# A new DRAM layout for the dense gates and for three weight matrices of an encoder block

## The chip, the core and the metric

One core of a Trainium2 chip runs the whole kernel in one launch. The metric is the device time of one execution in microseconds. TensorE (PE) multiplies, VectorE (DVE) and ScalarE (ACT) do the elementwise work, GpSimd (POOL) issues the gathers, SyncE (SP) issues the plain DMAs, and 16 DMA engines move the bytes of both queues: q0 holds what POOL issues, q1 what SP issues.

## The reference

The block takes 1024 tokens of width 1024 in float32:

```
h = rmsnorm(x, g_mix);  q, k, v, u, gv = split(h @ w_in)          # w_in 1024 x 2560
o = diff_attention(q, k, v)           # 4 heads, block-causal, softmax(1) - lam * softmax(2)
y = spatial_gating(gelu(u), gelu(gv)) # 128-position blocks, lower-triangular w_s
x = x + concat(o, y) @ w_out          # w_out 1024 x 1024
xn = rmsnorm(x, g_ffn)
s = (xn @ w_q) . sub_keys             # w_q 1024 x 2048; 8 heads x 2 halves x 128 keys
top 16 of each half -> top 16 pairs per head -> 128 (expert, gate) pairs per token of 16384 experts
x = x + sum_e gate_e * gelu(w_u[e] . xn) * w_v[e]
return rmsnorm(x, g_final)
```

## The kernel before

Tokens are eight blocks of 128, taken in four passes of two blocks. A front part (`front`) does everything up to the selection of experts. For each pass, stage A is the combined projection with `w_in`, B attention, M/Y the spatial gating, D the projection with `w_out` (line 509), S the queries with `w_q` (line 544) and the top 16 of each half, and t the selection of the pairs. Weights come in pieces of 128 partitions by 2 by 512 floats, 512 KB each, through a ring of three tiles (`pieces`, line 300): 80 loads of `w_in`, 32 of `w_out`, 64 of `w_q`.

The expert layer is done in two ways. Blocks 0, 1, 6 and 7 gather: 128 rows of `w_u` and then 128 rows of `w_v` for each token, one indirect DMA of 128 rows of 4 KB per pair index (line 664), and one DVE instruction of 1024 columns behind each (lines 685 and 699). Blocks 2 to 5 (512 tokens) are dense: all 16384 experts are multiplied, in 128 steps of 128 experts (`dense`), and a dense gate matrix picks those that were chosen.

The dense gates are built by `gates`, called G1 for blocks 2 and 3 and G2 for blocks 4 and 5. For each token two one-hot matrices (DVE lines 626 and 641, ACT lines 645 and 646) are multiplied on PE (line 650); ACT copies four tokens at a time into a tile `st` of 128 partitions by 128 expert columns by 16 tokens (line 651), and after four such copies SP stores `st` to the DRAM tensor `gd` (line 652). There are 32 stores of 1 MB, 16 in G1 and 16 in G2. G1 has one `st` tile and two `oh1` tiles, G2 has three `st` tiles (dictionaries G1 and G2, lines 46 and 47).

In `dense`, `gd` comes back in 16 loads of 2 MB into `gg` (line 750), one for each eight steps, double buffered. Each step loads 512 KB of `w_uT` (`ur`, line 757) and 512 KB of `w_v` (`vr`, line 777), splits both into a high and a low float32r part on ACT and DVE, makes `hp` on PE (lines 765 to 767), applies gelu and the gate (line 771) and accumulates the outputs (lines 743 to 745). Before it, four loads bring the transposed tokens into `xl` (line 724), and ACT and DVE split them (lines 726 and 727).

The order on each engine is fixed when the program is built: a scheduler interleaves the gathers with the front and with the dense steps, and every engine then runs its list in order and waits where it must. The `w_u` rows of blocks 0 and 1 and the `w_v` rows of block 0 are gathered in the front, the other gathers run beside the dense steps, and what is left of them after the last dense step is a tail.

Of the kernel before, what the change touches and what calls it, by code (L numbers as in the profile page):

```python
# [7 lines left out]
F32 = mybir.dt.float32  # L8
# [10 lines left out]
P = 128  # L19
# [19 lines left out]
TB = 16  # L39
NTB = TD // TB  # L40
GRP = 4
# [20 lines left out]
def peer_block(tc, d):  # L62
    nc = tc.nc
    dve, act, pe, pool, sp = nc.vector, nc.scalar, nc.tensor, nc.gpsimd, nc.sync

    with ExitStack() as ctx:
        E = ctx.enter_context
        cp = E(tc.tile_pool(name="consts", bufs=1))
        dram = E(tc.tile_pool(name="scratch", bufs=1, space=DRAM))
# [25 lines left out]
        S = {}  # L95
# [35 lines left out]
                                             op0=ALU.mult, op1=ALU.subtract)  # L131

        x1_d = [dram.tile([P, D], F32, name=f"x1_{b}") for b in range(NB)]
        gd = dram.tile([P, NTB, P, TB], F32, name="gd")
        xT_d = dram.tile([P, DC, TD], F32, name="xT_d")
        sel_t = {}
        rs2_t = {}
# [91 lines left out]
        def front():  # L229
# [151 lines left out]
            def stage_a(p, order):  # L381

                blocks = PASSES[p]
                nt = len(blocks) * P
                t0 = blocks[0] * P
                if ("xT", p) not in S:
                    S["xT", p] = norm_x(p)
                xT = S["xT", p]

                def natural(c):  # L390
                    ps = project(xT, lambda q: d["w_in"][:, q * 2:q * 2 + 2, c * 512:(c + 1) * 512], f"wi{p}_{c}", blocks)
                    for i, b in enumerate(blocks):
                        if c == 2:
                            act.activation(vv[b], ps[i], AF.Copy)
                        else:
                            t = a2.tile([P, 512], F32, name=f"ug{c}_{b}", tag=f"ug{c}", bufs=UG[c])
                            act.activation(t, ps[i], AF.Gelu_apprx_tanh)
                            S[c, b] = t
                def transposed(c):
                    ps = [accp.tile([P, 512], F32, name=f"qk{p}_{c}_{i}", tag="acc") for i in range(2)]  # L400
                    src = lambda q: d["w_in"][:, q * 2:q * 2 + 2, c * 512:(c + 1) * 512]
                    for dc, w in pieces(src, f"wi{p}_{c}", xT[1] is None):
                        for h in range(NH):
                            o_ = ps[h // 2][:, (h % 2) * nt:(h % 2) * nt + nt]
                            mm(o_, cut(w, slice(None), slice(h * P, (h + 1) * P)), cut(xT, slice(None), dc, slice(0, nt)),
                               dc == 0 and h % 2 == 0, dc == DC - 1, skip_group_check=True)
                    if c == 0:
                        S["q", p] = a2.tile([P, NH, PW * P], F32, name=f"qT{p}", tag="qT")
                        for h in range(NH):
                            act.activation(S["q", p][:, h, :nt], ps[h // 2][:, (h % 2) * nt:(h % 2) * nt + nt], AF.Copy,  # L410
                                           scale=HD ** -0.5 / SLOPES[h])
                    else:
                        for h in range(0, NH, 2):
                            act.activation(kT[:, h:h + 2, t0:t0 + nt],
                                           ps[h // 2][:, :2 * nt].rearrange("p (a b) -> p a b", a=2), AF.Copy)
                for c in order:
                    if c == "g":
                        gmlp(p, accp, "acc")
                    elif c in "01":
                        transposed(int(c))  # L420
                    else:
                        natural(int(c))
# [78 lines left out]
            def stage_d(p):  # L501

                blocks = PASSES[p]
                x1 = {b: f4.tile([P, D], F32, name=f"x1_{b}", tag="x4k") for b in blocks}
                for b in blocks:
                    sp.dma_start(x1[b], d["x"][b * P:(b + 1) * P, :])
                for hf in range(2):
                    hs = slice(hf * 512, (hf + 1) * 512)
                    ps = project(S["mT", p], lambda q: d["w_out"][:, q * 2:q * 2 + 2, hs], f"wo{p}_{hf}", blocks)
                    for i, b in enumerate(blocks):  # L510
                        dve.tensor_tensor(x1[b][:, hs], x1[b][:, hs], ps[i], ALU.add)
                sT = pair(f"sT{p}", f"S{p}")
                ms = sm.tile([P, PW], F32, name=f"ms2_{p}", tag="ms")
                for i, b in enumerate(blocks):
                    sp.dma_start(x1_d[b], x1[b])
                    jk = f2.tile([P, D], BF16, name=f"jk2_{b}", tag="jk", bufs=1)
                    act.activation(jk, x1[b], AF.Square, accum_out=ms[:, i:i + 1])
                rs2 = sel.tile([P, PW], F32, name=f"rs2_{p}", tag="rs2")
                dve.tensor_copy(rs2, rsqrt(ms, PW, 1.0 / D, f"rf{p}", sm))
                for i, b in enumerate(blocks):  # L520
                    rs2_t[b] = rs2[:, i:i + 1]
                    act.activation(x1[b], x1[b], AF.Copy, scale=rs2_t[b])
                    pp, tag = (accp, "acc") if p == len(PASSES) - 1 else (smp, "smp")
                    transpose_split(x1[b], gffn, sT[0], sT[1], i, pp, tag, f"sT{b}")
                S["sT", p] = sT
                if blocks[0] in DENSE:
                    c0 = DENSE.index(blocks[0]) * P
                    sp.dma_start(xT_d[:, :, c0:c0 + PW * P], sT[0])

            def stage_s(p):  # L530
# [8 lines left out]
                def query(c):  # L539

                    kt = f2.tile([P, 4, P], F32, name=f"kt{p}_{c}", tag="kt")
                    sp.dma_start(kt, d["keys"][:, c * 4:(c + 1) * 4, :])
                    ps = [accp.tile([P, 512], F32, name=f"pq{p}_{c}_{i}", tag="acc") for i in range(2)]
                    src = lambda q: d["w_q"][:, q * 2:q * 2 + 2, c * 512:(c + 1) * 512]
                    for dc, w in pieces(src, f"sc{p}_{c}", T[1] is None):
                        for q in range(4):
                            mm(ps[q // 2][:, (q % 2) * nt:(q % 2) * nt + nt], cut(w, slice(None), slice(q * P, (q + 1) * P)),
                               cut(T, slice(None), dc, slice(0, nt)), dc == 0 and q % 2 == 0, dc == DC - 1, skip_group_check=True)
                    qT = f2.tile([P, 4, PW * P], F32, name=f"sq{p}_{c}", tag="sq")
                    for q in range(0, 4, 2):  # L550
                        act.activation(qT[:, q:q + 2, :nt], ps[q // 2][:, :2 * nt].rearrange("p (a b) -> p a b", a=2), AF.Copy)
                    return kt, qT
# [45 lines left out]
        def gates(blocks, pp, tag, bufs):  # L598
# [7 lines left out]
            for b in blocks:  # L606
# [7 lines left out]
                for c in range(P // TB):  # L614
                    ci = bi * (P // TB) + c
                    st = g1.tile([P, P, TB], F32, name=f"st{ci}", tag="st", bufs=bufs["st"])
                    for t0 in range(0, TB, 4):
# [31 lines left out]
                        for j in range(4):  # L649
                            pe.matmul(pg[:, j * P:(j + 1) * P], oh2[:, j, :], oh1[:, j, :], start=True, stop=True)  # L650
                        act.activation(st[:, :, t0:t0 + 4], pg.rearrange("p (t i) -> p i t", t=4), AF.Copy)  # L651
                    sp.dma_start(gd[:, ci], st)
            gs.close()

        ring = [0]
# [53 lines left out]
        def dense():  # L709
# [37 lines left out]
            for gi in range(NG):  # L747
                if gi % 2 == 0:
                    gg = d2.tile([P, NTB, 2 * GRP, TB], F32, name=f"gg{gi}", tag="gg")
                    sp.dma_start(gg, gd[:, :, gi * GRP:(gi + 2) * GRP, :])  # L750
                vh = d1.tile([P, GRP, D], F32R, name=f"vh{gi}", tag="vh")
                vl = d1.tile([P, GRP, D], F32R, name=f"vl{gi}", tag="vl")
                av = []
# [67 lines left out]
def _layouts(inputs):  # L821

    import numpy as np
    c = np.ascontiguousarray

    def chunked(a):

        return c(a.reshape(-1, P, a.shape[-1]).transpose(1, 0, 2))
    i = {k: np.asarray(v) for k, v in inputs.items()}
    r = {}  # L830
    r["x"] = c(i["x"].reshape(NT, D))
    r["w_in"] = chunked(i["w_in"][0])
    r["w_out"] = chunked(i["w_out"][0])
    r["g_mix"] = c(i["g_mix"][0].reshape(DC, P).T)
    r["g_ffn"] = c(i["g_ffn"][0].reshape(DC, P).T)
    r["g_ffn_row"] = c(i["g_ffn"][0])
    r["g_final"] = c(i["g_final"])
    r["g_gv"] = c(i["g_gv"][0])
    r["g_subln"] = c(i["g_subln"][0].reshape(P, 1))
    r["g_gout"] = c(i["g_gout"][0].reshape(4, P).T)  # L840
    r["b_s"] = c(i["b_s"][0].T)
    r["lam"] = np.concatenate([i["lam_q1"][0], i["lam_k1"][0], i["lam_q2"][0], i["lam_k2"][0]])
    r["w_s"] = c(i["w_s"][0].transpose(2, 0, 1))
    r["w_q"] = chunked(i["peer_wq"][0])
    r["keys"] = c(i["peer_keys"][0].reshape(16, P, P).transpose(2, 0, 1))
    r["w_u"] = c(i["peer_wu"][0])
    r["w_v"] = c(i["peer_wv"][0])

    r["w_uT"] = c(i["peer_wu"][0].reshape(P, P, DC, P).transpose(0, 3, 2, 1).reshape(P, P, D))
    return r  # L850
# [19 lines left out]
```

## Time and profile before

| | us |
|---|---|
| median of 3 runs | 2809.84 |
| lowest, highest | 2806.77, 2818.14 |
| profiled execution | 2825.71 |
| its span, first to last instruction | 2823.9 |
| PE busy | 2423.6 (86%) |
| DVE busy | 2404.8 (85%) |
| ACT busy | 1000.3 (35%) |
| POOL busy | 1488.8 (53%) |
| DMA q0 (gathers), share of 16 engines | 53.0% |
| DMA q1 (SP's loads and stores), share of 16 engines | 33.2% |

A share over the whole span mixes stages with different limits, so the profile is to be read by stage. The front lasts to about 1300 us, the dense steps from there to about 2707 us, the tail to the end.

### The profile page before, as it was taken

How to read it: one execution, taken by the hardware profiler on the slowest of the kernel's cores; microseconds unless marked ns; L12 is line 12 of the kernel's file. 1: busy time of each engine (PE TensorE's matmuls, PEld its weight loads, DVE VectorE, ACT ScalarE, POOL GpSimd, SP SyncE). 2: the span in 40 equal slices, each digit the busy share in tenths (PEclk: the TensorE clock that was granted, in tenths of full speed). 3: DMA queues.
4: the chain of work that ended last, by engine and by line, in shares of the span. 5: the costliest groups of instructions: out<-in, count | busy, mean ns of one | idle time of the engine just before them, and what ended most of it. 6: DMA issues, size and time to landing. Idle time of an engine off the chain costs nothing.

```text
span 2823.9 us, 33571 instructions
## 1 busy us (share of the span) xinstructions
PE 2423.6 (86%) x10764; PEld 1909.5 (68%) x10764; DVE 2404.8 (85%) x5223; ACT 1000.3 (35%) x2063; POOL 1488.8 (53%) x1139
## 2 busy tenths in 40 slices
PE   6789997995569774797999999999999999999930
PEld 5575655753447542695887887888888888888820
DVE  4448867999988999999898887987888978888998
ACT  5553322224553542983323232232232322323300
POOL 5362564356655325321265646655566657655665
PEclk9799998996569777898999999999999999999965
DMA  5266999998899858797699999999999989998998
GB/s 174 59 181 184 343 365 359 337 339 297 299 348 331 295 182 290 264 366 247 214 346 350 352 322 366 354 333 342 328 356 343 342 306 384 349 359 303 331 333 343
DMA packets 316514, 869.56 MB, mean 308 GB/s; under 512 B 26033, under 2 KB 93745, under 8 KB 312241
## 3 DMA queue, kind: packets, MB, share of 16 engines
q0 software_dynamic: 149760, 545.33, 53.0%
q1 hardware_dynamic: 166576, 322.09, 33.2%
q8 instruction: 85, 1.39, 0.2%
q14 instruction: 93, 0.75, 0.1%
HBM read 823.28 MB, written 44.04 MB: 307 GB/s over the span
## 4 chain that ended last, share of the span: by engine, by line
PE 61%; DVE 19%; DMA 10%; issue 5%; ACT 4%; POOL 1%; SPq 0%; DVEq 0%; ACTq 0%; POOLq 0%
PE hp L765 7%; PE hp L767 7%; PE hp L766 7%; PE y L745 6%; PE y L743 6%; PE y L744 6%; PE pq L309 5%; DVE y L699 4%; DVE u L685 4%; DMA u<-in_w_u_dram,idx 3%; PE pgg L650 2%; PE wi L309 2%; PE op L743 2%; PE op L745 2%; PE op L744 2%
## 5 line engine op out<-in xcount | busy, mean ns | idle before, releaser
L664 POOL DMA_INDIRECT v<-in_w_v_dram,idx x512 | 664.9, 1299 | 656.5 <-DVE y L699 321.2
L664 POOL DMA_INDIRECT u<-in_w_u_dram,idx x512 | 700.1, 1367 | 530.7 <-DVE h L685 226.7
L699 DVE SCALAR_TENSOR_TENSOR y<-v,a,y 128x1024 f32<-128x1024 f32 x512 | 656.3, 1282 | 15.8 <-DMA v<-in_w_v_dram,idx 9.0
L685 DVE CUSTOM_DVE_ANT_0 u<-u,xn 128x1024 f32<-128x1024 f32 x512 | 614.2, 1220 | 50.6 <-DMA u<-in_w_u_dram,idx 50.2
L765 PE MATMUL hp<-xh,uh 128*128 128x512 f32 x1024 | 400.0, 391 | 22.0 <-ACT xh L726 15.6
L766 PE MATMUL hp<-xl,uh 128*128 128x512 f32 x1024 | 399.3, 390 | 2.4 <-DVE xl L727 2.4
L767 PE MATMUL hp<-xh,ul 128*128 128x512 f32 x1024 | 399.3, 390 | 0.6 <-DVE ul L761 0.6
L778 ACT ACTIVATE vh<-vr 128x1024 fp32r<-128x1024 f32 x128 | 130.7, 1052 | 510.8 <-PE op L745 481.1
L744 PE MATMUL y<-vl,ah 128*128 128x512 f32 x768 | 298.8, 389 | 0.0
L743 PE MATMUL y<-vh,ah 128*128 128x512 f32 x768 | 298.8, 389 | 0.0
L745 PE MATMUL y<-vh,al 128*128 128x512 f32 x768 | 287.6, 389 | 2.2 <-DVE al L775 2.2
L650 PE MATMUL pgg<-oh,oh 128*128 128x128 f32 x1024 | 190.3, 344 | 102.7 <-ACT st L651 63.9
L650 PEld LDWEIGHTS pgg<-oh,oh 128*128 128x128 f32 x1024 | 170.3, 247 | 132.6 <-ACT st L651 84.0
L765 PEld LDWEIGHTS hp<-xh,uh 128*128 128x128 f32 x1024 | 192.7, 188 | 64.4 <-ACT xh L726 15.8
L766 PEld LDWEIGHTS hp<-xl,uh 128*128 128x128 f32 x1024 | 192.7, 188 | 43.0 <-DVE xl L727 3.1
L767 PEld LDWEIGHTS hp<-xh,ul 128*128 128x128 f32 x1024 | 192.6, 188 | 41.4 <-DVE ul L761 1.4
L760 ACT ACTIVATE uh<-ur 128x1024 fp32r<-128x1024 f32 x128 | 135.1, 1056 | 168.7 <-PE hp L766 149.7
L761 DVE TENSOR_TENSOR ul<-ur,uh 128x1024 fp32r<-128x1024 f32 x128 | 156.3, 1221 | 36.6 <-ACT uh L760 36.5
L309 PE MATMUL pq<-sT,sc 128*128 128x256 f32 x768 | 184.0, 389 | 0.7 <-ACT sT L127 0.7
L779 DVE TENSOR_TENSOR vl<-vr,vh 128x1024 fp32r<-128x1024 f32 x128 | 153.5, 1220 | 16.3 <-ACT vh L778 16.3
L745 PEld LDWEIGHTS y<-vh,al 128*128 128x128 f32 x768 | 144.2, 188 | 33.3 <-DVE al L775 3.5
L309 PEld LDWEIGHTS pq<-sT,sc 128*128 128x128 f32 x768 | 143.8, 195 | 32.8 <-issue 10.7
(440 smaller groups left out, 4117.2 us busy)
## 6 DMA issues: line engine op xcount, KB each, us to landing
ur<-in_w_uT_dram SPq DMA_DIRECT2D x128, 512.0 KB, 6.5
vr<-in_w_v_dram SPq DMA_DIRECT2D x128, 512.0 KB, 6.5
wi<-in_w_in_dram SPq DMA_DIRECT2D x80, 512.0 KB, 5.0
sc<-in_w_q_dram SPq DMA_DIRECT2D x64, 512.0 KB, 6.4
gd<-st SPq DMA_DIRECT2D x32, 1024.0 KB, 7.2
gg<-gd SPq DMA_DIRECT2D x16, 2048.0 KB, 21.8
wo<-in_w_out_dram SPq DMA_DIRECT2D x32, 512.0 KB, 7.0
x<-in_x_dram SPq DMA_DIRECT2D x16, 512.0 KB, 6.5
```

Source lines behind the costliest of these rows:

```text
L309: pe.matmul(ps, s_[i], m_[j], start=first and n == 0, stop=last and n == len(ops) - 1, **kw)
L650: pe.matmul(pg[:, j * P:(j + 1) * P], oh2[:, j, :], oh1[:, j, :], start=True, stop=True)
L664: pool.indirect_dma_start(out=t, out_offset=None, in_=d[src], in_offset=bass.IndirectOffsetOnAxis(ap=ix, axis=0))
L685: dve.tensor_tensor_reduce(t, t, xn, 1.0, 0.0, ALU.mult, ALU.add, h[:, j:j + 1])
L699: dve.scalar_tensor_tensor(y, t, a[:, j:j + 1], y, op0=ALU.mult, op1=ALU.add)
L743: pe.matmul(ps, ah[:, bs], vh[:, hs], start=first, stop=False, skip_group_check=True)
L744: pe.matmul(ps, ah[:, bs], vl[:, hs], start=False, stop=False, skip_group_check=True)
L745: pe.matmul(ps, al[:, bs], vh[:, hs], start=False, stop=last, skip_group_check=True)
L761: dve.tensor_tensor(ul, ur, uh, ALU.subtract)
L765: pe.matmul(hp[:, :TD], uh[:, ds_], xh[:, dc, :], start=(dc == 0), stop=False)
L766: pe.matmul(hp[:, :TD], uh[:, ds_], xl[:, dc, :], start=False, stop=False)
L767: pe.matmul(hp[:, :TD], ul[:, ds_], xh[:, dc, :], start=False, stop=(dc == DC - 1))
```

## The change

Only the order of bytes in DRAM changes. In `gd` the expert columns are grouped by eight: one partition's data for one load of `gg` lies in one run of 16 KB, where it was 32 runs of 512 B. The store of `st` writes 16 runs of 512 B for each partition, 16 KB apart, where it wrote one run of 8 KB. `w_in`, `w_out` and `w_q` are laid out on the host so that one load reads 4 KB per partition in one run, where it read two runs of 2 KB. The number of DMAs and the bytes of each stay as they were.

```
-        gd = dram.tile([P, NTB, P, TB], F32, name="gd")
+        gd = dram.tile([P, P // (2 * GRP), NTB, 2 * GRP, TB], F32, name="gd")
...
-                    ps = project(xT, lambda q: d["w_in"][:, q * 2:q * 2 + 2, c * 512:(c + 1) * 512], f"wi{p}_{c}", blocks)
+                    ps = project(xT, lambda q: d["w_in"][:, c, q * 2:q * 2 + 2, :], f"wi{p}_{c}", blocks)
...
-                    ps = project(S["mT", p], lambda q: d["w_out"][:, q * 2:q * 2 + 2, hs], f"wo{p}_{hf}", blocks)
+                    ps = project(S["mT", p], lambda q: d["w_out"][:, hf, q * 2:q * 2 + 2, :], f"wo{p}_{hf}", blocks)
...
-                    src = lambda q: d["w_q"][:, q * 2:q * 2 + 2, c * 512:(c + 1) * 512]
+                    src = lambda q: d["w_q"][:, c, q * 2:q * 2 + 2, :]
...
-                    sp.dma_start(gd[:, ci], st)
+                    sp.dma_start(gd[:, :, ci], st.rearrange("p (a b) t -> p a b t", b=2 * GRP))
...
-                    sp.dma_start(gg, gd[:, :, gi * GRP:(gi + 2) * GRP, :])
+                    sp.dma_start(gg, gd[:, gi // 2])
...
-    def chunked(a):
-
-        return c(a.reshape(-1, P, a.shape[-1]).transpose(1, 0, 2))
+
+    def tiled(a):
+
+        return c(a.reshape(-1, P, a.shape[-1] // 512, 512).transpose(1, 2, 0, 3))
...
-    r["w_in"] = chunked(i["w_in"][0])
-    r["w_out"] = chunked(i["w_out"][0])
+    r["w_in"] = tiled(i["w_in"][0])
+    r["w_out"] = tiled(i["w_out"][0])
...
-    r["w_q"] = chunked(i["peer_wq"][0])
+    r["w_q"] = tiled(i["peer_wq"][0])
```

No instruction moves on any engine. SP's list at the end of G2 and the entry of the dense part, in the changed kernel (a row is a line of the kernel, the tile written, the tile read, and the shape of the transfer):

```order
L652 DMA gd<-st_8550 2048x1x128
L300 DMA sc_3_2_9019<-in_w_q_dram 128x1024
L707 DMA out_dram<-y_18507 128x1024
L542 DMA kt_3_8995<-in_keys_dram 128x512
L300 DMA sc_3_3_9029<-in_w_q_dram 128x1024
L750 DMA gg_9219<-gd 128x4096
L757 DMA ur_9223<-in_w_uT_dram 128x1024
L777 DMA vr_9261<-in_w_v_dram 128x1024
L757 DMA ur_9265<-in_w_uT_dram 128x1024
L777 DMA vr_9303<-in_w_v_dram 128x1024
L750 DMA gg_9761<-gd 128x4096
L724 DMA xl<-xT_d 128x1024 x4
```

The kernel before has the same rows in the same places; the shapes there are 128x2048 for `gd<-st`, 128x2x512 for the `sc` loads and 128x32x128 for `gg<-gd`. Two loads of `gg` stand ahead of the loads of `xl`, in both.

## Rows read from the trace of the kernel before

**Rows 1.** Windows by stage: length, engines' busy us (instructions), clock, DMA share, GB/s.

```profile
0.00:240.00 240.00, 188.70 (x1048) 157.19 (x1049) 115.44 (x509) 124.82 (x303) 115.67 (x100) 0.88 0.47 139
240.00:500.00 260.00, 234.95 (x840) 146.87 (x839) 203.31 (x616) 79.51 (x211) 130.20 (x104) 0.95 0.92 332
680.00:1040.00 360.00, 268.58 (x1150) 199.13 (x1151) 325.72 (x888) 178.22 (x477) 174.01 (x139) 0.74 0.84 298
1130.00:1270.00 140.00, 122.91 (x766) 111.40 (x765) 138.41 (x362) 123.50 (x330) 45.03 (x38) 0.94 0.88 314
1270.00:1300.00 30.00, 12.18 (x68) 10.23 (x66) 29.79 (x156) 8.87 (x12) 1.81 (x1) 0.72 0.99 328
1300.00:2707.00 1407.00, 1397.51 (x6142) 1153.14 (x6142) 1221.06 (x1637) 407.54 (x522) 811.41 (x577) 1.00 0.92 331
2707.00:2824.00 117.00, 0.00 (x0) 0.00 (x0) 106.24 (x109) 5.64 (x10) 69.86 (x67) 0.51 0.89 349
```

**Rows 2.** DVE's waits for gathers, 1300 to 2710: total us, times, longest.

```profile
DVE u L685 <- DMA u<-in_w_u_dram,idx: 10.6, 14, 1.5
DVE y L699 <- DMA v<-in_w_v_dram,idx: 6.8, 3, 5.5
```

**Rows 3.** Two links of the chain, dense part: start, us, what.

```profile
1483.46 20.03 DMA vr<-in_w_v_dram
...
1739.56 23.75 DMA ur<-in_w_uT_dram
```

**Rows 4.** PE's wait at the dense entry (us, times, longest); DVE there, by time.

```profile
PE hp L765 <- ACT xh L726: 15.6, 1, 15.6
...
1299.49 1.28 DVE L727 TENSOR_TENSOR xl<-xl,xh 128x512 fp32r<-128x512 f32 x2
```

**Rows 5.** The page's DMA issues: count, size, median us from issue to landing.

```profile
ur<-in_w_uT_dram SPq DMA_DIRECT2D x128, 512.0 KB, 6.5
...
wi<-in_w_in_dram SPq DMA_DIRECT2D x80, 512.0 KB, 5.0
sc<-in_w_q_dram SPq DMA_DIRECT2D x64, 512.0 KB, 6.4
gd<-st SPq DMA_DIRECT2D x32, 1024.0 KB, 7.2
gg<-gd SPq DMA_DIRECT2D x16, 2048.0 KB, 21.8
wo<-in_w_out_dram SPq DMA_DIRECT2D x32, 512.0 KB, 7.0
```

**Rows 6.** Windows: 1 KB stores, 8 KB stores, 512 B loads, 4 KB gathers.

```profile
465.00:472.00 7.00, 7.00 (x34) 6.17 (x33) 3.11 (x16) 3.52 (x5) 3.45 (x3) 1.00 0.94 291
1002.00:1004.00 2.00, 2.00 (x11) 1.15 (x10) 2.00 (x5) 1.25 (x5) 0.46 (x1) 1.00 1.02 426
1290.00:1295.00 5.00, 0.00 (x0) 0.00 (x0) 5.00 (x25) 0.00 (x0) 0.00 (x0) 0.50 0.93 273
...
2720.00:2800.00 80.00, 0.00 (x0) 0.00 (x0) 78.42 (x74) 1.82 (x4) 58.32 (x56) 0.50 0.97 378
```

**Rows 7.** The chain from 230 to 500 us, shares by line.

```profile
by line: PE wi L309 13.7%; DMA u<-in_w_u_dram,idx 9.6%; PE qk L309 8.0%; DMA wi<-in_w_in_dram 6.5%; DVE u L685 6.0%; DMA wo<-in_w_out_dram 5.9%; PE s L444 5.6%; PE wo L309 5.0%; DMA x<-x 4.5%; PE pq L309 4.5%; issue 2.7%; PE ops L477 2.2%; 
```

**Rows 8.** G1's stores, 680 to 1040: issues, who waited, landing; DVE's wait for PE.

```profile
L652 SPq DMA_DIRECT2D gd<-st x16: 319/326/418, 682.5 to 1034.4; - x16
...
  ACT st L651: 26.9, 9
...
DMA to landing us min/median/max: 3.8/7.4/9.1
...
DVE oh L641 <- PE pgg L650: 4.7, 5, 1.4
```

**Rows 9.** G2's stores, 1130 to 1270: issues and landing.

```profile
L652 SPq DMA_DIRECT2D gd<-st x16: 319/324/460, 1133.4 to 1260.2; - x16
...
DMA to landing us min/median/max: 3.8/7.0/14.1
```

More of the change, by code (lines that the diff above doesn't have):

```diff
@@ L400, in transposed @@
                     ps = [accp.tile([P, 512], F32, name=f"qk{p}_{c}_{i}", tag="acc") for i in range(2)]
-                    src = lambda q: d["w_in"][:, q * 2:q * 2 + 2, c * 512:(c + 1) * 512]
+                    src = lambda q: d["w_in"][:, c, q * 2:q * 2 + 2, :]
                     for dc, w in pieces(src, f"wi{p}_{c}", xT[1] is None):
```

## The prediction

> **What bounds the kernel now.** I read the windows by stage first, since the shares of the whole span hide the stages. From 1300 to 2707 us PE is busy 1397.5 of 1407 us at the full clock [rows 1]: the dense steps are bound by PE, and 9.5 us of idle PE is all that any other engine or transfer takes there. From 2707 on PE has nothing and DVE is busy 106 of 117 us [rows 1]: the tail is the gathers left over, at DVE's pace. Before 1300 the picture changes. From 680 to 1300 DVE leads, with 325.7 of 360, 138.4 of 140 and 29.8 of 30 us [rows 1]. From 240 to 500 no engine is full, PE 235 and DVE 203 of 260 us, while the DMA engines are at 0.92. From 0 to 240 the DMA engines are at 0.47 and nothing is full [rows 1].
>
> The DMA share invites a wrong reading: 0.92 over the whole dense part looks like a bound. Whether it is one is seen in DVE's waits for gathers. They come to 10.6 and 6.8 us in 1410 us [rows 2], and the number of gathers left for the tail is fixed by DVE's list, not by how early they land. So spare bandwidth beside the dense steps buys at most those 17.4 us, and only where the wait holds up PE or the tail.
>
> **The change, part by part.** All 224 transfers (176 weight loads, 32 stores and 16 loads of `gd`) stay in their places on SP; only the sizes of their pieces change. So each part is a price per transfer, then what of it reaches the path.
>
> Prices. The share and the rate of a short stretch give what the 16 engines would move if full. In the tail 4 KB pieces move at 378 GB/s with a share of 0.97, so 390; 512 B loads at 273 with 0.93, so 294; 1 KB stores (`xT_d`) at 291 with 0.94, so 310; 8 KB stores of `gd` (the one issued at about 1001 us) at 426 with 1.02, so 418 [rows 6]. The first 240 us, where most loads have 2 KB pieces, give 139 / 0.47 = 296 [rows 1].
>
> (a) Weights, 176 loads of 0.524 MB. 1.77 us of the DMA engines each at 296 GB/s, 1.34 at 390: 0.43 us less. In the first 240 us the engines stand idle half the time; I take 1 us there, for the loads that begin the chain. From 230 to 500 the chain holds 6.5% + 5.9% of waiting for `wi` and `wo`, 33 us of 270 [rows 7]. If these landed faster in the ratio of the two rates, 24%, that would be 8 us; but a load of the same size that comes in 4 KB pieces already, `ur`, takes 6.5 us to land, against 5.0, 6.4 and 7.0 for `wi`, `sc` and `wo` [rows 5], so most of a landing is not piece size. I take 2 us. Against a gain stands that larger pieces give q1 a larger part of the busy engines, and the gathers beside it a smaller one. Sum -3 us; bounds -10 and +3.
>
> (b) Stores of G1. The store in 512 B pieces is not in the trace. Nearest rows: 1 KB stores at 310 and 512 B loads at 294 GB/s, so 1.05 MB takes 3.4 to 3.6 us of full engines, against 2.5 at 418: +1.0 us. Beside gathers it is worse: a `gg` load in 512 B pieces lands in 21.8 us for twice the bytes, 10.9 per MB, against 7.2 for a `gd` store [rows 5], +3.7. G1 has one `st` tile, so ACT's first copy of the next 16 tokens waits for the store. Queued behind that copy are ACT's next one-hots, PE's next gate product and what stands behind it on PE. Now 9 of 16 stores hold ACT up, 26.9 us in all, while DVE waits only 4.7 us for gate products [rows 8], about 17%. The cushion: the stores come every (1034.4 - 682.5) / 15 = 23.5 us, 5.9 for a group of four tokens, and two `oh1` tiles let DVE be up to two groups ahead, 11.7 us. With +1.0 to +3.7 us on 16 stores ACT waits 16 to 59 us more; 17% of it is 3 to 10. I take +5 us; bounds 0 (all in the cushion) and +20 (a third comes through).
>
> The Trainium skill has a rule for this price (DMA: Bandwidth & Descriptors, section Why small descriptors are slow): each packet costs a fixed three cycles or so beside its 32-byte beats. An estimate from that page: 19 cycles for 512 B, so 152 for 4 KB in eight pieces, against 131 in one, 16% more. The trace does not agree in size: 390 against 294 GB/s is 33% [rows 6]. By the page's figure the store would cost 0.4 us more instead of 1.0, and this term +2.
>
> (c) Stores of G2. 16 stores in 126.8 us, one every 8.5 us, and three tiles, so a tile is wanted again after about 25 us while a store lands in 7.0, at most 14.1 [rows 9]: no wait. The engines are what is short: they are busy 0.88 x 140 = 123 us [rows 1], and the stores add 16 x 1.0 = 16, about all that is free. The `sc` loads in the same queue feed PE and, through the top 16, DVE, which has 1.6 us of idle time in 140. I take +2 us; bounds -2 (the `sc` loads gain more than the stores cost) and +11.
>
> (d) Entry of the dense part. PE stands still for 15.6 us until ACT has `xh` [rows 4], and two `gg` loads are queued ahead of `xl`. Each needs 2.1 MB / 294 = 7.1 us of full engines, and 5.4 at 390: `xl` could land 3.5 us earlier. It helps little, since the second product needs the low part from DVE, and DVE is busy 29.8 of the 30 us before it takes it up at 1299.5 in its own order [rows 1, 4]. The last store lands later by 1 to 4 us, ahead of all this. I take 0; bounds -3.5 and +3.
>
> (e) Dense steps. The 14 other `gg` loads keep q1 for about 20 us each; a `ur` or `vr` behind one lands after 20.0 or 23.8 us instead of 6.5, and the chain runs through it [rows 3, 5]. With 16 KB pieces `gg` has the larger part of the engines and should be through in half the time. Of the 9.5 us of idle PE I take back 4; bounds 0 and -9.5. What hides the rest of the saved DMA time is PE's own work, at 99%.
>
> (f) Tail: no `gg`, no weights, DVE's pace. 0.
>
> Sum: -3 + 5 + 2 + 0 - 4 = 0, against the profiled execution's 2825.7 us (span 2823.9). The runs shown have a median of 2809.84, 15.9 us lower; the sum carries over as a difference: 2810 us. The ends add to -25 and +37.
>
> **The rivals.**
>
> Faster: the dense part is bound by DMA after all. For it: a share of 0.92 with gathers in flight all the time. 16 loads give back 16 x (7.1 - 5.4) = 27 us of DMA time, and DVE's 17.4 us of waiting for gathers [rows 2] would go and come off the tail, as its list runs ahead. Against it: PE at 99%. Time: 2810 - 17 = 2793 us.
>
> Slower: the stores cost much more than loads of the same pieces. Place: G1's single tile and the full engines in G2. If 512 B stores move at half of 294 GB/s, a store takes 7.1 us instead of 2.5 and lands 4.6 us later alone, and over 14 us later beside gathers. It decides from the point at which a G1 store lands after about 12 us, DVE's two groups. Then perhaps a third of 16 x 7 us of ACT's extra waiting reaches DVE, +35, of which 5 are in the sum; and G2's 16 x 4.6 = 74 us of extra DMA time meets 17 us of room, of which perhaps a quarter of the excess is felt, +12. Time: about 2850 us; the milder case, from where the cushion starts to fail, 2825 to 2840. For it: the one-tile ring, and the chain that already passes through these stores. Against it: 1 KB stores show no sign of it [rows 6].
>
> The Trainium skill has a rule on this side (DMA: Bandwidth & Descriptors, section Latency and other measured facts): rows that lie a large power of two apart in HBM copied at 207 GB/s and less, and padding restored the rate. The new pieces are 16 KB apart, the partitions 256 KB. The loads of `gg` before, 8 KB apart with the same partition distance, moved at 294 GB/s, so the trace does not bear it out for reads; no run here shows it yet for stores.
>
> That the change doesn't do what it says, the large runs being moved in pieces as small as now, would leave 2810 us and counts with the forecast.
>
> **How the numbers follow.** About 0.5%, 14 us, is what a measurement can tell from no change here. Forecast, the terms nearly cancel: 0.55. Faster by the DMA-bound dense part or by (a) and (e) at their ends: 0.20. Slower by the stores: 0.25, of which about 0.08 beyond 2840. The range 2790 to 2840 takes in the sum of the gains to -20 and of the costs to +30. Below 2795.8 is faster, above 2823.9 slower.
>
> **What would show it.** Right: PE busy 99% of the dense part again; `gg` landing in about 10 us; `ur` and `vr` never waiting over 15 us; `gd` landing in 8 to 11 us in G1, with ACT waiting 40 to 80 us for it and DVE under 15 for gate products; the dense part beginning within 10 us of 1300; the tail at 117 us. Wrong: a tail shorter by over 10 us (the faster rival), or a dense part that begins over 15 us later with DVE idle between 680 and 1270 (the slower one).

## The result, and the profile after

The changed kernel takes 2835.16 us (median of five runs, 2828.36 to 2840.25), the kernel before 2811.77 in the same five rounds: a ratio of 1.0073, 95% interval 1.0053 to 1.0092, so 15 to 26 us slower. The profiled execution of after took 2838.12 us with a span of 2836.3, only 12.4 us more than the profiled one of before, but that one lay 14 us above its own median. So these two traces are used for places, waits and the lengths of single stages, and the size of the whole comes from the timed runs.

The windows of after, with the bounds of [rows 1] as far as the entry, the dense part and the tail moved with it (length, busy us and instructions of PE, PEld, DVE, ACT, POOL, clock, DMA share, GB/s):

```profile
0.00:240.00 240.00, 188.57 (x1044) 157.66 (x1045) 113.44 (x491) 124.62 (x303) 115.65 (x100) 0.88 0.46 139
240.00:500.00 260.00, 238.21 (x856) 150.42 (x856) 208.50 (x644) 80.33 (x214) 135.20 (x105) 0.94 0.91 336
680.00:1040.00 360.00, 244.72 (x1063) 180.19 (x1063) 301.50 (x810) 165.88 (x449) 158.25 (x132) 0.75 0.82 281
1130.00:1270.00 140.00, 116.38 (x705) 102.89 (x704) 139.86 (x300) 127.10 (x344) 54.00 (x42) 0.91 0.93 309
...
1317.00:2719.00 1402.00, 1398.13 (x6142) 1155.54 (x6142) 1220.75 (x1636) 406.65 (x520) 813.97 (x576) 1.00 0.90 331
2719.00:2836.00 117.00, 0.00 (x0) 0.00 (x0) 106.38 (x109) 5.64 (x10) 69.87 (x67) 0.51 0.89 349
```

One row stands out. From 680 to 1040 DVE is busy 301.5 us where it was 325.7, with 78 fewer instructions, and PE, ACT, POOL and the DMA share fell too: by 1040 some 24 us of DVE's and PE's work is still to be done. The other stages are as before to within some five us of busy time, and to within nine from 1130 to 1270, a window that G2 now reaches some 18 us later.

The stores of G1 (all 16, and who waited for them; then those from 680 to 900 alone), in after:

```profile
L652 SPq DMA_DIRECT2D gd<-st x16: 512/519/525, 680.0 to 1056.7; - x16
...
  ACT st L651: 64.0, 12
...
DMA to landing us min/median/max: 5.2/8.5/15.6
...
L652 SPq DMA_DIRECT2D gd<-st x9: 513/519/525, 680.0 to 857.4; - x9
...
DMA to landing us min/median/max: 5.6/14.1/15.6
```

The 16 stores, first to last issue, took 376.7 us against 351.9 [rows 8]: 24.8 more. The median landing rose only from 7.4 to 8.5 us, but the longest from 9.1 to 15.6, and the late ones lie together: 14.1 us is the median of the nine before 900. The waits of DVE and of ACT there (total us, times, longest):

```profile
ACT st L651 <- DMA gd<-st: 64.0, 12, 11.9
...
DVE oh L641 <- PE pgg L650: 15.9, 10, 5.5
DVE oh L641 <- issue: 13.4, 2, 10.6
```

DVE's waits for one-hot tiles come to 29.3 us where they were 5.3, the 4.7 of [rows 8] and 0.6 put down to "issue". The 24.0 more are about as much as the whole lengthening of G1 in these two traces. What the profile calls "issue" in the second row is the same wait, as one such place shows. The timeline from 774 to 798 (start, duration, what, and in brackets the wait before it):

```profile
774.12 0.60 DVE L641 TENSOR_SCALAR oh<-iota,gT 128x128 f32<-128x128 f32 x2
...
776.63 0.51 SPq L652 DMA_DIRECT2D gd<-st  x1
...
777.70 0.59 DVE L641 TENSOR_SCALAR oh<-iota,gT 128x128 f32<-128x128 f32 x2
...
781.11 0.59 DVE L641 TENSOR_SCALAR oh<-iota,gT 128x128 f32<-128x128 f32 x2
...
784.26 0.08 DVE L685 DVE_READ_ACCUMULATOR2_ANT h<- 128x1 f32 x1
...
792.12 0.60 ACT L651 ACTIVATE st<-pgg 128x512 f32<-128x512 f32 x1 [11.88 <-DMA gd<-st]
...
792.77 2.08 PE L650 MATMUL pgg<-oh,oh 128*128 128x128 f32 x8 [14.04 <-ACT st L651]
...
794.94 0.60 DVE L641 TENSOR_SCALAR oh<-iota,gT 128x128 f32<-128x128 f32 x2 [10.60 <-issue]
...
797.56 1.84 POOL L664 DMA_INDIRECT u<-in_w_u_dram,idx  x1 [12.01 <-DVE ry_t L113]
```

The store is issued at 776.63 and lands 15.5 us later. DVE writes two more groups of one-hots (777.70, 781.11) and a little else until 784.34, 7.7 us after the issue. Then both `oh1` tiles are full, and DVE stands still until the store lands, ACT copies, and PE's product of 792.77 to 794.85 frees a tile. POOL, whose next gather needs DVE, stands with it. The chain of waits from 660 to 900 goes the same way. It passes through six stores, three of them over 14 us long (start, us, what):

```profile
by line: DMA gd<-st 27.9%; DMA u<-in_w_u_dram,idx 13.9%; PE pgg L650 12.4%; DVE u L685 8.3%; PE pq L309 7.5%; ACT st L651 5.4%; issue 5.3%; PE s L444 3.6%; DVE oh L626 2.5%; DVE oh L641 2.3%; POOL u L664 1.6%; PE wo L309 1.5%; ACT rg3j L338
...
680.01 14.78 DMA gd<-st
...
718.66 14.14 DMA gd<-st
...
776.63 15.46 DMA gd<-st
```

Before, stores were 11.6% of that chain, and a store of that stretch landed in 9.1 us at most [rows 8]. G2's stores in after, 1130 to 1290, answer to [rows 9]:

```profile
L652 SPq DMA_DIRECT2D gd<-st x16: 513/525/526, 1151.3 to 1279.3; - x16
...
who waited for it (us, times):
...
DMA to landing us min/median/max: 5.2/9.8/16.1
```

They land later (9.8 against 7.0 us) and nobody waits: 128.0 us from first to last, 126.8 before. The page's DMA issues, which answer to [rows 5], and the dense part's gate instructions:

```profile
ur<-in_w_uT_dram SPq DMA_DIRECT2D x128, 512.0 KB, 6.6
...
wi<-in_w_in_dram SPq DMA_DIRECT2D x80, 512.0 KB, 5.7
sc<-in_w_q_dram SPq DMA_DIRECT2D x64, 512.0 KB, 6.0
gd<-st SPq DMA_DIRECT2D x32, 1024.0 KB, 8.7
gg<-gd SPq DMA_DIRECT2D x16, 2048.0 KB, 10.6
wo<-in_w_out_dram SPq DMA_DIRECT2D x32, 512.0 KB, 6.3
```

```profile
L771 DVE TENSOR_TENSOR ga<-ga,gg x128: 679/686/700, 1332.7 to 2700.8; 128x512 f32<-128x512 f32 x128
```

`gg` lands in half the time, 10.6 us for 21.8, as the change should give. The 128 dense steps took 1368.1 us from the first gate to the last, and PE stood idle 3.9 of 1402 us where it was 9.5 of 1407. The weights are no faster: `wi` 5.7 for 5.0, `sc` 6.0 for 6.4, `wo` 6.3 for 7.0.

### The profile page after: what moved, and what is told of

Its sections match the earlier page's. It is cut to its first block, busy times and chain, and to the rows that moved or that the text cites. A ratio compares the mean times of both kernels' runs of the same rounds, so it can differ in the third digit from the quotient of the medians.

```text
span 2836.3 us, 33571 instructions
## 1 busy us (share of the span) xinstructions
PE 2415.8 (85%) x10764; PEld 1906.4 (67%) x10764; DVE 2404.7 (85%) x5223; ACT 1000.5 (35%) x2063; POOL 1483.8 (52%) x1139
## 4 chain that ended last, share of the span: by engine, by line
PE 57%; DVE 18%; DMA 10%; issue 9%; POOL 3%; ACT 3%; SPq 0%; POOLq 0%; DVEq 0%; ACTq 0%
PE hp L767 7%; PE hp L765 7%; PE hp L766 7%; PE pq L309 6%; PE y L745 5%; PE y L743 5%; PE y L744 5%; DMA u<-in_w_u_dram,idx 4%; DVE y L699 4%; DMA gd<-st 4%; DVE u L685 4%; PE pgg L650 3%; PE op L745 2%; PE op L744 2%; PE op L743 2%
## 5 line engine op out<-in xcount | busy, mean ns | idle before, releaser
L685 DVE CUSTOM_DVE_ANT_0 u<-u,xn 128x1024 f32<-128x1024 f32 x512 | 614.8, 1221 | 56.7 <-DMA u<-in_w_u_dram,idx 55.5
L765 PE MATMUL hp<-xh,uh 128*128 128x512 f32 x1024 | 400.9, 392 | 14.6 <-ACT xh L726 11.4
L650 PE MATMUL pgg<-oh,oh 128*128 128x128 f32 x1024 | 183.1, 335 | 131.9 <-ACT st L651 97.2
L650 PEld LDWEIGHTS pgg<-oh,oh 128*128 128x128 f32 x1024 | 163.6, 238 | 160.1 <-ACT st L651 123.1
L765 PEld LDWEIGHTS hp<-xh,uh 128*128 128x128 f32 x1024 | 193.3, 189 | 56.0 <-ACT xh L726 11.6
L744 PEld LDWEIGHTS y<-vl,ah 128*128 128x128 f32 x768 | 144.1, 188 | 29.9
## 6 DMA issues: line engine op xcount, KB each, us to landing
gg<-gd SPq DMA_DIRECT2D x16, 2048.0 KB, 10.6
```

What stands on the lines that cost most here:

```text
L685: dve.tensor_tensor_reduce(t, t, xn, 1.0, 0.0, ALU.mult, ALU.add, h[:, j:j + 1])
L744: pe.matmul(ps, ah[:, bs], vl[:, hs], start=False, stop=False, skip_group_check=True)
L765: pe.matmul(hp[:, :TD], uh[:, ds_], xh[:, dc, :], start=(dc == 0), stop=False)
```

## The experiments

Theory 1: the loss comes from G1's stores in 512 B pieces, which land late beside the gathers and hold up G1's one `st` tile. Rivals: the weights; G2 and the entry of the dense part; the engine time that small pieces take from the gathers, whatever the tiles. Ratios are to the kernel before, timed on the same chip.

**One part at a time.** The gates alone (the three weight matrices as before, five lines back), and the weights alone (the three lines on `gd` back):

```
 e1: src = lambda q: d["w_q"][:, q * 2:q * 2 + 2, c * 512:(c + 1) * 512]     # likewise w_in, w_out
 e2: sp.dma_start(gd[:, ci], st);  sp.dma_start(gg, gd[:, :, gi * GRP:(gi + 2) * GRP, :])
```

> Only the layout of the gates is changed; the weights stay in 2 KB runs. Theory 1 (the one st tile of G1: its stores land late beside gathers, ACT waits, then DVE): slower by 18 to 28 us, ratio 1.006 to 1.010; DVE level with before at 680 us and 20 us or more behind by 880; G2 adds nothing; some 4 us come back in the dense part. Rival (the weights' larger pieces take bandwidth from the gathers, and that is the loss): no slower than before, ratio 0.997 to 1.001.

> Only the weights are laid out in 4 KB runs. Theory 1: faster by 1 to 5 us, ratio 0.998 to 1.000, DVE ahead by 2 to 4 us at 680 and from there on. Rival (weights against gathers): slower by about 20 us, ratio 1.007.

e1: 1.0068 (1.0045 to 1.0091). e2: 1.0003 (0.9989 to 1.0016). The gates carry the loss, the weights neither gain nor lose. e2's trace has the dense part with unchanged loads of `gg`:

```profile
L771 DVE TENSOR_TENSOR ga<-ga,gg x128: 672/683/740, 1308.7 to 2674.7; 128x512 f32<-128x512 f32 x128
```

That is 1366.0 us, less than after's 1368.1. The 1372.8 us of the trace of before were thus not the layout's: it was an execution with a long dense part.

**Which stores.** e3 stores blocks 2 and 3 (G1) in the old runs of 8 KB and blocks 4 and 5 (G2) in the new layout, e4 the other way round; each load of `gg` becomes two of 1 MB.

```
+  gd2 = dram.tile([P, P // (2 * GRP), NTB // 2, 2 * GRP, TB], F32, name="gd2")
+  if ci < NTB // 2:  sp.dma_start(gd[:, ci], st)                                            # e4: >=
+  else:  sp.dma_start(gd2[:, :, ci - NTB // 2], st.rearrange("p (a b) t -> p a b t", b=2 * GRP))
+  sp.dma_start(gg[:, :NTB // 2], gd[:, :, gi * GRP:(gi + 2) * GRP, :])
+  sp.dma_start(gg[:, NTB // 2:], gd2[:, gi // 2])
```

> The weights as in the change; G1's gates (blocks 2 and 3) stored in 8 KB runs as before, G2's in 512 B runs as in the change; each load of gg is two of 1 MB, one in 512 B and one in 8 KB runs. Theory 1: G1's loss is gone, so 2 to 9 us faster than before, ratio 0.997 to 0.9995, ACT's waiting for G1's stores about 27 us again. Rival (the DMA time of any 512 B store, G1 and G2 alike): half of the loss stays, 8 to 12 us slower than before, ratio 1.003 to 1.004.

> The mirror of the run with G1 in 8 KB runs: G1's gates stored in 512 B runs, G2's in 8 KB runs, weights as in the change. Theory 1: all of the loss is here, 15 to 25 us slower than before, ratio 1.005 to 1.009, ACT waiting 55 to 75 us for G1's stores. Rival (DMA time of any 512 B store): 8 to 12 us slower, ratio 1.003 to 1.004.

e3: 0.9980 (0.9961 to 0.9998), 2808.72 us, faster than both kernels by a little. e4: 1.0047 (1.0031 to 1.0063), slower than before; the ratio is just under the 1.005 to 1.009 that Theory 1 asked, and ACT's waiting, 50.6 us, under its 55 to 75. G1's stores, e3 first:

```profile
L654 SPq DMA_DIRECT2D gd<-st x16: 319/326/382, 685.1 to 1035.8; - x16
...
  ACT st L652: 21.4, 10
...
DMA to landing us min/median/max: 3.9/5.9/11.5
```

```profile
L656 SPq DMA_DIRECT2D gd<-st x16: 512/519/548, 679.8 to 1045.3; - x16
...
  ACT st L652: 50.6, 11
...
DMA to landing us min/median/max: 4.8/8.1/16.6
```

G1's layout sets whether ACT waits 21 or 51 us and whether the stretch is 350.7 or 365.5 us. G2's new layout costs nothing that e3 can tell.

**The size of the pieces.** 32 or 16 expert columns in a group in place of eight: stores in 2 KB (e5) or 1 KB pieces (e6), loads of `gg` in 512 B as before.

```
+  gd = dram.tile([P, P // (8 * GRP), NTB, 8 * GRP, TB], F32, name="gd")       # e6: 4 * GRP
+  sp.dma_start(gd[:, :, ci], st.rearrange("p (a b) t -> p a b t", b=8 * GRP))
+  sp.dma_start(gg, gd[:, gi // 8, :, gi % 8 * GRP:gi % 8 * GRP + 2 * GRP, :])
```

> As the change, but gates grouped by 32 experts: G1 and G2 store in 2 KB pieces, gg is loaded in 512 B pieces as before. Theory 1 (a store in more pieces is passed by more gather packets and lands later; one st tile passes that on): stores in G1 from 680 to 900 land in 7 to 9 us, DVE loses 0 to 6 us there, gg still lands after about 20 us; ratio to before 0.999 to 1.003. Rival (any store that is not one 8 KB run is slow): G1 lands as late as in the change (14 us), ratio 1.007 or more.

> As the change, but gates grouped by 16 experts: stores in 1 KB pieces, gg in 512 B pieces as before. Theory 1: stores in G1 from 680 to 900 land in 8 to 12 us, DVE loses 6 to 15 us there, nothing comes back in the dense part; ratio 1.002 to 1.006. Rival (the loss goes by the store's own DMA time, which by the rates is nearly the same for 1 KB and 512 B): as much lost in G1 as in the change, 20 to 25 us, and nothing back, ratio 1.008 to 1.010.

e5: 1.0006 (0.9987 to 1.0025). e6: 1.0031 (1.0018 to 1.0045). G1 in all these runs, from the same three views (660 to 1062 us; one trace each, so a stretch is good to a few us):

| | store pieces in G1 | ACT waits for stores: total, longest | DVE waits for one-hot tiles | first to last store | ratio |
|---|---|---|---|---|---|
| before | 8 KB | 26.9, 4.5 | 5.3 | 351.9 | |
| e3 | 8 KB | 21.4, 4.1 | 5.0 | 350.7 | 0.9980 |
| e5 | 2 KB | 41.7, 7.5 | 11.9 | 352.7 | 1.0006 |
| e6 | 1 KB | 47.0, 8.4 | 17.0 | 363.6 | 1.0031 |
| e4 | 512 B | 50.6, 10.3 | 20.7 | 365.5 | 1.0047 |
| e1 | 512 B | 52.8, 10.7 | 20.0 | 373.5 | 1.0068 |
| e10 | 512 B | 56.7, 12.0 | 25.7 | 370.4 | 1.0068 |
| after | 512 B | 64.0, 11.9 | 29.3 | 376.7 | 1.0073 |

All columns grow together as the pieces shrink, but the loss does not begin at once: at 2 KB ACT waits 14.8 us more than before and DVE 6.6, and G1 is as long as it was (+0.8 us, within what a trace can tell). Where ACT's longest wait is 8.4 us and more, the stretch grows by 12 to 25 us.

**The loads of `gg` alone.** Stores as before, weights as in the change, and `gg` filled with 2 MB of `w_v` in runs of 16 KB; the gates that are stored are not read.

```
-  sp.dma_start(gg, gd[:, :, gi * GRP:(gi + 2) * GRP, :])
+  sp.dma_start(gg.rearrange("p a b t -> p (a b t)"), d["w_v"].rearrange("(g p r) d -> g p (r d)", p=P, r=4)[gi])
```

> Weights as in the change; stores of the gates as before (8 KB); each load of gg reads 2 MB of w_v in 16 KB runs in place of the gates, so the dense blocks are weighted by other numbers, and the loads don't depend on the stores. Theory (gg in large pieces lets ur and vr land in time): PE's waits in the dense part fall by 3 to 6 us, the whole is 3 to 8 us faster than before, ratio 0.997 to 0.999. Rival (the dense part is bound by PE and hides gg anyway): ratio 0.9995 to 1.0005. Rival (the dense part is bound by DMA): 15 us or more faster, ratio 0.995 or less.

0.9993 (0.9978 to 1.0008): most of the expected 0.997 to 0.999 was missed. In its trace:

```profile
L771 DVE TENSOR_TENSOR ga<-ga,gg x128: 677/684/745, 1303.3 to 2669.0; 128x512 f32<-128x512 f32 x128
...
DMA to landing us min/median/max: 10.1/10.7/19.7
```

The loads land in 10.7 us (22.5 in e2), and the dense steps take 1365.7 us against e2's 1366.0. Twice as fast a load is worth nothing that these runs can tell.

**Fewer bytes beside the stores.** `w_u` rows of block 1 gathered as 1 KB instead of 4 KB, with the old layouts (e8) and the change's (e9).

```
+  thin = src == "w_u" and b == 1
+  pool.indirect_dma_start(out=t[:, 0:256] if thin else t, out_offset=None,
+                          in_=d[src].rearrange("e (f c) -> (e f) c", f=4) if thin else d[src],
```

> The control: the kernel before, but each gather of block 1's w_u rows, which run beside G1, brings 128 rows of 1 KB in place of 4 KB (the dot product is taken of that quarter four times, so block 1's result is another). The scheduler sets another order in the front. Both theories: 0 to 15 us faster than before (ratio 0.994 to 1.000), G1's stores land in 4 to 8 us.

> The same thinned gathers (128 rows of 1 KB for block 1's w_u) with the layouts of the change, instruction for instruction in the order of the control. Theory 1 (the 512 B stores land late because gather packets pass them): with a quarter of the gather bytes G1's stores land in 5 to 9 us and the two kernels are within 5 us of each other, ratio of the two 0.998 to 1.002. Rival (a store in 512 B pieces is slow by itself, with no traffic beside it): the stores land in 10 us or more as in the change, and this one is 15 to 25 us slower than the control, ratio of the two 1.005 to 1.009.

e8: 1.0088 (1.0065 to 1.0111). e9: 1.0134 (1.0113 to 1.0156). Both totals missed. The scheduler made another order, in which G1 runs from about 770 to 1135 and stands mostly beside full gathers of `w_v`. The pair differs by 0.46%, some 13 us, which fits neither theory. Stretch by stretch it says more. In e9:

```profile
720.00:820.00 100.00, 40.27 (x158) 31.68 (x158) 95.82 (x218) 41.34 (x128) 60.20 (x49) 0.57 0.51 157
820.00:1060.00 240.00, 197.91 (x866) 141.64 (x866) 214.05 (x597) 110.20 (x285) 93.16 (x85) 0.83 0.84 287
```

Its first four stores, issued from 774.3 to 822.1 where the DMA engines are half idle, land in 5.3 to 7.9 us, though in 512 B pieces, and the same four in e8 go from 772.4 to 819.6: 47.8 us against 47.2. From there to the last store of G1 e9 takes 313.2 us and e8 303.3; the share is 0.84 up to 1060 in e9. So small pieces did not delay these four stores, where the engines were half idle, and the loss lies where they are full. But ACT's longest wait for a store of G1 is only 5.3 us in e9 (6.6 in e8), and G1 grew by some 10 us all the same, which long waits do not explain. Where the gathers run was not set by the experiment as intended, so this pair shows the place and leaves the way open.

**The change once more**, with e8 and e9.

> The change itself beside runs of before on this chip, for the comparison with the partial versions: ratio 1.005 to 1.009 as first measured; G1's stores from 680 to 900 land in 9 to 15 us; PE's waits in the dense part after 1340 under 4 us.

1.0068 (1.0043 to 1.0092).

**Two tiles in G1.** To give G1 two tiles in the same memory, the tiles were halved: 8 tokens each, two in G1, six in G2, 64 stores of 512 KB.

```
-TB = 16
+TB = 8
-G1 = dict(st=1, ...); G2 = dict(st=3, ...)
+G1 = dict(st=2, ...); G2 = dict(st=6, ...)
+  gd = dram.tile([P, P // (4 * GRP), NTB, 4 * GRP, TB], F32, name="gd")       # e12: [P, NTB, P, TB], as before
```

> The change with st tiles of half the size: 8 tokens in place of 16, two tiles in G1 where there was one, six in G2 where there were three, so the memory they take is the same; 64 stores of 512 KB. Sixteen expert columns are grouped, so a store still writes pieces of 512 B (16 columns by 8 tokens); gg is then read in runs of 256 B, half those of the kernel before. The scheduler sets another order than in the two kernels, but the same one here and in e12, so the pair is what counts. Theory 1 (a store in small pieces lands late beside gathers, and the loss comes from G1's single tile, which stops ACT until the store has landed): ACT fills one tile while the other lands, it waits under 25 us for stores from 660 to 1060 in place of 64, and this kernel stands 0.998 to 1.003 to e12. Rival (the small pieces cost by themselves, since they take engine time from the gathers beside them, whatever the tiles): 1.005 to 1.009 to e12, as the change to the kernel before.

> The control of e11: the same half tiles and the same order on every engine, weights as in the change, but gd in its old layout, so a store writes runs of 4 KB per partition and a load of gg reads pieces of 256 B. Both theories: ACT waits under 25 us for stores from 660 to 1060; the time is set by the other order and by 32 more stores, 0.995 to 1.004 to the kernel before. Only its distance to e11 tells the two apart.

e11: 1.0284 (1.0261 to 1.0306). e12: 1.0293 (1.0270 to 1.0315). The totals missed 0.995 to 1.004 by far. The last gate of the dense steps stands in e11 at 2684.4 us of a span of 2888.2, so 204 us are left behind it, against 135 in before (2688.7 of 2823.9): the new order leaves more gathers to the tail. But the pair, with the same order on every engine, does not differ: 512 B pieces take 0.9991 of the time of 4 KB runs (0.996 to 1.002, the two intervals put together as roots of squares), against 1.0068 and 1.0073 with one tile. G1's stores, e11 and then e12:

```profile
L652 SPq DMA_DIRECT2D gd<-st x32: 512/513/525, 666.9 to 1002.3; - x32
...
  ACT st L651: 3.1, 1
```

```profile
L652 SPq DMA_DIRECT2D gd<-st x32: 319/320/327, 686.0 to 1019.8; - x32
```

ACT waits 3.1 us in e11 and not at all in e12. The stretches are 335.4 and 333.8 us, 1.6 us apart where one tile made it 24.8, and both are shorter than G1 of before. This decides against the rival of engine time: the same bytes go out in the same pieces beside gathers, and with a second tile they cost next to nothing in G1. The traces with one tile agree: DVE's waits for gathered `w_u` rows in G1 (660 to 1062 us) did not grow, 14.8 us in before and 12.7, 8.5 and 12.1 in after, e1 and e10. A store of half the size may also land sooner, and these two traces give no landing; how much of the cure is that, and how much the second tile, is not told apart.

## Why the prediction was right and wrong

The forecast was 2810 us, no change; the change is slower by 15 to 26 us. The time lies within the range, and it is that of the milder slower case, 2825 to 2840. The range held it by the room that was left for that rival; the sum behind 2810 did not. Of the signs named, `gg` in about 10 us, ACT's 40 to 80 us of waiting and PE's 99% came true. But DVE waited 29.3 us for gate products where it should have been under 15, and the dense part began 16.8 us later with DVE idle in G1, which was the sign of the slower rival.

**(b), G1's stores: right place, wrong size, and this is the step that failed.** The term was +5 us, bounds 0 and +20; G1 lengthened by 24.8 us in the trace of after, 21.6 in e1, 18.5 in e10. Its first half held. The price alone was taken at +1.0 us. A store that runs almost by itself in after moves at 350 GB/s, so 3.0 us for its 1.05 MB, against 2.5 at the 426 GB/s of the 8 KB store [rows 6]: +0.5 us. Its window (length, busy us of PE, PEld, DVE, ACT and POOL, clock, DMA share, GB/s):

```profile
1042.00:1045.00 3.00, 0.00 (x0) 0.00 (x0) 3.00 (x11) 2.45 (x6) 0.94 (x1) 0.60 1.22 350
```

Divided by the share, as the prediction did, that is 287 GB/s and +1.1 us. But a share of 1.22 is more time than the 16 engines have, so packets overlap in it, and the quotient is no rate that bytes moved at. Two of the prediction's own rates came from windows that mix pieces. In before, from 465 to 472 (the gathers' queue: packets, MB, share) and from 1290 to 1295 (all packets):

```profile
q0 software_dynamic: 350, 1.30, 62.2%
...
DMA packets 1626, 1.37 MB, mean 273 GB/s; under 512 B 30, under 2 KB 1473, under 8 KB 1626
```

Of the 2.03 MB moved in the window of "1 KB stores" 1.30 were gathers, and of the 1.37 MB of "512 B loads" at most 1473 x 512 B = 0.75 were in 512 B pieces. So 310 and 294 GB/s are not prices of such pieces. For the sum that did little harm, since +1.0 us lies above what the lone store shows.

ACT's extra waiting was put at 16 to 59 us and is 37.1 in after, 25.9 in e1, 29.8 in e10. What failed is "17% of it". DVE's waits grew by 24.0 us for ACT's 37.1: 65%. Two things account for that; they are read from the waits, and no run sets the cushion by itself.

First, 17% was the share of short waits, none over 4.5 us. The cushion takes a wait whole or up to its own length; what is over goes through whole. e5 fits the one side (14.8 us more of ACT's waiting, 0.8 us of G1), after the other; e9 with its short waits does not fit.

Second, the cushion was worked out as 11.7 us from the mean spacing of all groups, 5.9 us, and its end set at a landing of 12 us. In the stretch that matters DVE's one-hots come every 3.4 to 3.6 us (774.12, 777.70, 781.11), and DVE stops 7.7 us after the issue. They came as densely before, at the same place:

```profile
766.74 0.60 DVE L641 TENSOR_SCALAR oh<-iota,gT 128x128 f32<-128x128 f32 x2
...
770.31 0.59 DVE L641 TENSOR_SCALAR oh<-iota,gT 128x128 f32<-128x128 f32 x2
...
773.73 0.60 DVE L641 TENSOR_SCALAR oh<-iota,gT 128x128 f32<-128x128 f32 x2
```

[rows 8] already had a landing of 9.1 us in G1: nothing was left of the cushion, and that could be read before.

The landing too was judged by a typical price, +3.7 us beside gathers. The median over G1 rose by 1.1 us, but from 680 to 900 by 6.2 (7.9 to 14.1 in the trace of after; 10.0 in e1, 9.7 in e10), and it is the late ones that pay.

**(a), weights:** -3 taken, 0 measured (e2, 0.9989 to 1.0016, so -3 to +4 us); within the bounds. That most of a landing is not piece size fits: with larger pieces the landings went both ways (5.0 to 5.7, 7.0 to 6.3).

**(c), G2:** +2 taken, no wait in the trace, and e3 with the new G2 is not slower. Three tiles and 25 us until one is wanted again cover a landing of 16.1 us.

**(d), entry:** PE's wait for `xh`, 15.6 us before [rows 4], is 11.4 in after. The last store of G1 came 22.3 us later than before and the first gate 16.8 us, so about 5 us came back in between; how much of that is the `gg` loads and how much slack in G2 stays open.

**(e), dense steps:** the mechanism was there (`gg` in 10.6 us, PE's idle time 9.5 to 3.9), but the 4 us taken from it were read from one execution. e2, with the old loads, has as short a dense part, and e7 gives 0.9978 to 1.0008. By runs the term is 0, at most 6 us. **(f), tail:** DVE 106.38 us in 117, as before.

**The rivals.** Faster: fallen. DVE's waits for gathers in the dense part are 15.6 + 8.4 us in after, where they were 17.4 [rows 2], and e7, with the `gg` loads this rival asks for and no late store, gains at most 6 us. Slower: its place (the one-tile ring) and its point of decision, a landing of about 12 us, were near the truth; its price, half rate, was not (350 GB/s), nor its G2 part. What was held against it, that 1 KB stores show no sign, came from the mixed window. The trace of before had such a store in G1's stretch, 1 MB of `xT_d` in 1 KB pieces:

```profile
L528 SPq DMA_DIRECT2D xT_d<-sT x1: 550/550/550, 851.1 to 851.1; - x1
...
DMA to landing us min/median/max: 15.7/15.7/15.7
```

It landed after 15.7 us, twice the 7.4 of the 8 KB stores [rows 8]. Nobody waited for it, so it cost nothing, and the other store of this kind, issued at 460.3, landed after 8.1; but it is a sign of the kind that was looked for. That the change doesn't do what it says is excluded by `gg` at 10.6 us.

The Trainium skill's figure for small packets (DMA: Bandwidth & Descriptors, section Why small descriptors are slow) would have made the term +2. By the mixed windows the prediction found 33% where the estimate from that rule was 16%; the lone store's 350 GB/s against 426 in 8 KB pieces is 22% more time, not far from it. Its rule on rows a large power of two apart (same page, section Latency and other measured facts) was weighed as a danger for the stores. It states 207 GB/s for rows 512 KiB apart; here the partitions lie 256 KB apart and the lone store moves at 350 GB/s, so no run here bears it out, and none goes to the distances of that rule.

**Open.** e4 has G1's 512 B stores like the change and may have lost less, 1.0047 (up to 1.0063) against 1.0073 (from 1.0053); its pieces lie 8 KB apart instead of 16, and whether that matters was not tried. The pieces of e6 and e5 lie 32 and 64 KB apart and lost less than the change, so distance alone does not order the losses. Why the late landings gather before 900 in after is shown only as far as the share of the DMA engines goes (e9). A version of e11 with an order that keeps the tail short was not made.

## What to carry to other kernels

A layout moves cost between writer and reader; ask which of the two has slack. Here the reader (`gg`, double buffered, one load for eight steps) had plenty and the writer (one `st` tile) had little, so the writer should keep its large pieces, as in e3; that G2's new layout gains something there is not shown (e3's 0.9961 to 0.9998 and e2's 0.9989 to 1.0016 overlap). For a ring of one tile, work the cushion out at the densest place and set it against the longest landing, not the median: a share of waits that got through before says nothing once a wait is longer than the cushion.

## What was not expected of the hardware

The same 1 MB store in 512 B pieces lands in 5.2 us or in 15.6 in one stage of after, and in e9 the stores issued where the DMA engines are half idle are among the early ones, while a 2 MB load made of large runs went from 21.8 to 10.6 us beside the same gathers. And executions with the same loads in the dense part differ by 5 to 7 us there (1372.8 in before; 1366.0 in e2, 1367.4 in e5): a term of that size can't be read from one trace.
